# Layer 1's feed-forward in a two-layer latent backbone: where VectorE reads the high parts of weights, which engine splits the down weights, and when the second half's operands are made

## The chip, the core and the metric

The kernel runs on one NeuronCore of a Trainium2 chip. The metric is the device time of one execution in microseconds (us). A core has five engines that run side by side, each through its own list of instructions in order, and wait for each other on semaphores: TensorE (PE in the profile; its weight loads are PEld), VectorE (DVE), ScalarE (ACT), GpSimd (POOL) and SyncE (SP), which here does nothing but start transfers (DMAs) from memory. SBUF is the core's working memory; PSUM is the memory of eight banks into which TensorE accumulates, and which VectorE and ScalarE read and write as well.

## The reference

Two layers over 1024 latent tokens of width 1024 (and 256 context tokens). Each layer is a mixer and a feed-forward, with an RMS norm and a modulation by a conditioning vector ahead of each. Layer 0's mixer is Fourier mixing beside windowed attention, layer 1's is neighbourhood attention. The change is in layer 1's feed-forward, with a hidden width of 2816:

```
def _swiglu(h, wg, wu, wd):
    return (jax.nn.silu(h @ wg) * (h @ wu)) @ wd
...
h = _rms(x, norm2_g[i]) * (1.0 + sc2) + sh2
x = x + g2 * _swiglu(h, ffn_w_gate[i], ffn_w_up[i], ffn_w_down[i])
```

## The kernel before

**Precision.** Every matrix product is made of three: each operand is split in a high part (rounded to a short mantissa, type `F32R`) and a low part (what the rounding left), and `mm3` issues high by high, high by low and low by high (L74, L75, L76). So each weight tile needs a cast to the high part and a subtraction for the low one. In layer 1's feed-forward `parts_of` does this for a 128x512 block: ScalarE casts (`w_hi`, L1238), then VectorE, or GpSimd where told so, subtracts (`w_lo`, L1239). Both results lie in rings of 6 blocks.

**The stage.** It comes last in the kernel, behind layer 1's attention and its output projection (`out_proj1`). The 1024 tokens are worked in two halves (`ci` 0 and 1) of 512, and each half in 22 column blocks `f` of 128 hidden units.

For a block, `gate_up1` multiplies with gate and up weights together. The weights are seen as a two by two block matrix (`b11`, `b21` the two halves of the gate weights' rows, `b12`, `b22` those of the up weights), the activations too (two halves of tokens by two halves of the 1024 inputs), and the product is made of seven block products in place of eight (Winograd's form of Strassen's scheme). GpSimd forms four combinations of the raw weights (`t1` to `t4`, L1323, L1324, L1328, L1332; tiles named `t` in the profile, in a ring of 4). Seven weight operands (`b11`, `t2`, `t3`, `t1`, `t4`, `b21`, `b22`, in this order) go through `parts_of`, the last two with GpSimd as the subtracting engine. Each product (`product7`) is 12 matmuls into a PSUM tile `p_ps`, of which there are 4. ScalarE copies the first product to `p` (L1326); VectorE adds up the others (`u`, `av`, `sg`, L1330 to L1351), ScalarE applies SiLU, and the result is split in `act_hi` and `act_lo` (L1353, L1354). The activations' own seven combinations, `c_hi` and `c_lo`, are made once for each half by `combine`.

Two blocks make a pair. After each even `f` from 2 on, `down1` multiplies the pair before it with its down weights: 8 tiles `d_ps` of 6 matmuls each, which VectorE adds into `x` (L1379). The down weights of a block come in two halves, each a transfer to `wd_raw` (L1368, a ring of 2), a cast on ScalarE (L1369) and a subtraction on VectorE (L1370); the parts lie in the rooms `h_hi` and `h_lo` (one pair each), which held the mixer's output before.

The raw gate and up weights (`w_raw`, L1232, 512 KB each) have a ring of 4, so those of block `f` can be fetched only once the last reader of block `f - 2` is done: for the gate weights that is the `b21` subtraction, for the up weights the `b22` one, both on GpSimd. SP issues all these transfers in one list. It waits in place when a buffer isn't free, and what stands behind it waits too.

**The two halves.** The norm of the second half (`norm1s`, handed on as `own1`) is a generator: each `gate_up1` advances it by some steps, amid the first blocks of the first half. Its results go to memory (`h_d`) and come back as `h_in` for `combine` between the last two downs of the first half.

**What sets the order.** In this stage nobody writes out each engine's list. The language's scheduler makes it from the order of the code and its own costs, within the dependencies and the rings.

Of the kernel before, what the change touches and what calls it, by code (L numbers as in the profile page):

```python
# [9 lines left out]
F32 = mybir.dt.float32  # L10
# [6 lines left out]
P = 128  # L17
# [46 lines left out]
def build(tc, io):  # L64
# [4 lines left out]
    def fl(ap):  # L69
        return ap.bitcast(F32)  # L70
# [1152 lines left out]
    ww, ww_cm = pools.open("ring1", bufs=6)  # L1223
    wk, wk_cm = pools.open("wk1")
    pd, pd_cm = pools.open("pd1", bufs=3, psum=True)
    pm, pm_cm = pools.open("pm1", bufs=1, psum=True)
    pp, pp_cm = pools.open("pp1", bufs=4, psum=True)
    HT = 256

    def raw_weights(src):  # L1230
# [3 lines left out]

    def parts_of(src, eng=V):

        hi, lo = (ww.tile([P, 4, P], F32R, name=n) for n in ("w_hi", "w_lo"))
        S.copy(hi, src)  # L1238
        eng.tensor_tensor(lo, src, fl(hi), ALU.subtract)  # L1239
        return hi, lo  # L1240

    def out_weights(dt):
# [24 lines left out]
    def norm1s(ci, adder, done):  # L1267


        ts = slice(ci * 512, ci * 512 + 512)  # L1270
        ss = wk.tile([P, 512], F32, name="nrm_ss")
        for i, k in enumerate(reversed(range(KT))):
            if i == 0:
                S.activation(ss, x[:, k, ts], AF.Square)
            else:
                sq = wk.tile([P, 512], F32, name="nrm_sq", tag="t", bufs=4)
                S.activation(sq, x[:, k, ts], AF.Square)
                adder.tensor_tensor(ss, ss, sq, ALU.add)
            yield
        for r in norm_rstd(ss, 512, wk, pm):  # L1280
            yield
        for i in range(4):
            both = []
            for k in (i, i + 4):
                t = wk.tile([P, 512], F32, name="nrm_t", tag="t", bufs=4)
                V.scalar_tensor_tensor(t, x[:, k, ts], nA[3][:, k, 0:1], r, ALU.mult, ALU.mult)
                h = wk.tile([P, 512], F32, name="nrm_h", bufs=2)
                S.activation(h, t, AF.Identity, bias=vec(1, 3)[:, k, 0:1], scale=1.0)
                both.append(h)
                yield  # L1290
            done(i, *both)
            yield
# [1 line left out]

    M1, M2 = slice(0, HT), slice(HT, 2 * HT)

    def combine(i, h0, h4, pool=wk, tags=("act_hi", "act_lo")):

        s, r = (pool.tile([P, 2, HT], F32, name="s_sum", tag=t, bufs=4) for t in tags)
        G.tensor_tensor(s[:, 0], h0[:, M2], h4[:, M2], ALU.add)  # L1300
        G.tensor_tensor(s[:, 1], s[:, 0], h0[:, M1], ALU.subtract)
        G.tensor_tensor(r[:, 0], h0[:, M1], h0[:, M2], ALU.subtract)
        G.tensor_tensor(r[:, 1], h4[:, M1], s[:, 1], ALU.subtract)
        for sl, src in ((slice(0, 1), h0[:, M1].unsqueeze(1)),
                        (slice(1, 3), h4.rearrange("p (a n) -> p a n", a=2)), (slice(3, 5), s), (slice(5, 7), r)):
            S.copy(c_hi[:, sl, i], src)
            V.tensor_tensor(c_lo[:, sl, i], src, fl(c_hi[:, sl, i]), ALU.subtract)
# [7 lines left out]
    def gate_up1(f, side=iter(())):  # L1315
        g, u = raw_weights(io["w_gate"][1, f]), raw_weights(io["w_up"][1, f])
        b11, b21, b12, b22 = g[:, 0:4], g[:, 4:8], u[:, 0:4], u[:, 4:8]
        t1, t2, t3, t4 = (wk.tile([P, 4, P], F32, name=n, tag="t", bufs=4) for n in ("t1", "t2", "t3", "t4"))
        p1, u2, u3, sg = (wk.tile([P, HT], F32, name=n) for n in ("p1", "u2", "u3", "sg"))
        av = wk.tile([P, 2, HT], F32, name="av", bufs=2)  # L1320
        hi, lo = (wk.tile([P, 512], F32R, name=n, bufs=4) for n in ("act_hi", "act_lo"))
        w = parts_of(b11)
        G.tensor_tensor(t1, b12, b11, ALU.subtract)  # L1323
        G.tensor_tensor(t2, b22, t1, ALU.subtract)  # L1324
        ps = product7(w, 0)
        S.copy(p1, ps)  # L1326
        w = parts_of(t2)
        G.tensor_tensor(t3, b22, b12, ALU.subtract)  # L1328
        ps = product7(w, 4)
        V.tensor_tensor(u2, ps, p1, ALU.add)  # L1330
        w = parts_of(t3)
        G.tensor_tensor(t4, t2, b21, ALU.subtract)  # L1332
# [5 lines left out]
        V.tensor_tensor(u2, ps, u2, ALU.add)  # L1338
        w = parts_of(t4)
        ps = product7(w, 2)  # L1340
        V.tensor_tensor(u3, u3, ps, ALU.subtract)
# [4 lines left out]
        V.tensor_tensor(sg, ps, p1, ALU.add)  # L1346
        S.activation(sg, sg, AF.Silu)
        w = parts_of(b22, G)
        ps = product7(w, 6)
        V.tensor_tensor(u2, ps, u2, ALU.add)  # L1350
        V.tensor_tensor(av[:, 0], u2, sg, ALU.mult)  # L1351
        avf = av.rearrange("p a n -> p (a n)")
        S.copy(hi, avf)  # L1353
        V.tensor_tensor(lo, avf, fl(hi), ALU.subtract)  # L1354
        advance(side, 3)
        return hi, lo


# [4 lines left out]
    def down_weights1(f):  # L1363

        w_in = w_room[f // 2 % 2]
        for h in range(2):
            raw = wk.tile([P, 4, P], F32, name="wd_raw", bufs=2)
            nc.sync.dma_start(raw, io["w_down"][1, f][:, 4 * h:4 * h + 4])  # L1368
            S.copy(w_in[:, f % 2, h, 0], raw)  # L1369
            V.tensor_tensor(w_in[:, f % 2, h, 1], raw, fl(w_in[:, f % 2, h, 0]), ALU.subtract)  # L1370

    def down1(ci, fs, acts, last):
        w_in = w_room[fs[0] // 2 % 2]
        ts = slice(ci * 512, ci * 512 + 512)
        for dt in range(KT):
# [3 lines left out]
            V.scalar_tensor_tensor(x[:, dt, ts], ps, vec(1, 5)[:, dt, 0:1], x[:, dt, ts], ALU.mult, ALU.add)  # L1379
            if last:  # L1380
                nc.scalar.dma_start(io["out"][:, dt, ts], x[:, dt, ts])

    def keep(i, h0, h4):
        for k, h in ((i, h0), (i + 4, h4)):
# [11 lines left out]
    for ci in range(2):  # L1396
        acts = {}
        for f in range(NF):
            if f:
                down_weights1(f - 1)  # L1400
            acts[f] = gate_up1(f, own1)
            if f % 2 == 0 and 2 <= f < NF - 2:
                down1(ci, (f - 2, f - 1), [acts.pop(f - 2), acts.pop(f - 1)], False)
        down_weights1(NF - 1)
        for f in (NF - 4, NF - 2):
            down1(ci, (f, f + 1), [acts.pop(f), acts.pop(f + 1)], f == NF - 2)
            if f == NF - 4 and ci == 0:
                for i in range(4):
                    h = wr.tile([P, 2, 512], F32, name="h_in", tag="w_raw")
                    for n in range(2):  # L1410
                        nc.sync.dma_start(h[:, n], h_d[:, i + 4 * n])
                    combine(i, h[:, 0], h[:, 1], wr, ("w_raw", "w_raw"))
    pools.close(pp_cm, pm_cm, pd_cm, wk_cm, ww_cm, wr_cm, xp_cm, cc_cm, bg_cms[1], cst_cm)

# [109 lines left out]
```

## Time and profile before

| | |
|---|---|
| time, median of 3 runs | 2990.45 us (2989.44 to 2991.74) |
| the profiled execution | 2985.47 us; from first to last instruction 2983.6 us |
| mean granted TensorE clock | 0.988 of full speed |
| TensorE busy | 2837.0 us, 95% of the span |
| VectorE, ScalarE, GpSimd busy | 57%, 35%, 25% of the span |
| the stage: first block product to the end | 2190.6 to 2983.6 us |

The profile names an instruction by its line, its engine and its tiles, written out<-in. "Idle before" is the time in which the engine had nothing to do ahead of an instruction, with the instruction or transfer that released it. Over the whole kernel VectorE and GpSimd are far from full; in this stage VectorE is busy for 654 of 794 us. The stage falls into the blocks of the first half (to 2564 us), its last two downs (to 2597 us), the blocks of the second half (to 2957 us) and the last two downs.

### The profile page before, as it was taken

The page shows a single profiled execution, that of the slowest core. Times are in us where ns is not written, and L with a number is a line of the kernel's source. Part 1 is how long each engine was busy: PE and PEld are TensorE (multiplying, and loading weights), DVE is VectorE, ACT ScalarE, POOL GpSimd, SP SyncE. Part 2 cuts the span into 40 slices and gives each one's busy share as a digit, 9 for nine tenths or more (in the row PEclk, how much of TensorE's full clock was granted, in tenths as well). Part 3 has the DMA queues.
Part 4 walks back from the last instruction along what each step waited for, and adds up shares of the span by engine and source line. Part 5 has one row for each costly group of instructions (what it writes and reads, how often), then busy time and mean ns, then how long its engine had stood idle before and what let it go on. Part 6 is the DMA issues. An engine that isn't in the chain of part 4 may idle for free.

```text
span 2983.6 us, 43968 instructions
## 1 busy us (share of the span) xinstructions
PE 2837.0 (95%) x16874; PEld 2355.5 (79%) x16874; DVE 1692.7 (57%) x3172; ACT 1051.9 (35%) x2135; POOL 732.1 (25%) x738
## 2 busy tenths in 40 slices
PE   7989999999999999999989999999989899889999
PEld 5876768888888888888767887777778788778888
DVE  5775553622323333333575242666488787888887
ACT  4345552511111111111353232666354333433332
POOL 1112332000000000000220003554155454554452
PEclk9989999999999999999999999999999999999999
DMA  7236664111011111011134236873543222322221
GB/s 273 94 106 236 216 218 129 57 43 40 31 44 43 36 36 43 29 43 43 57 113 145 85 103 174 196 181 89 182 137 110 87 85 96 128 95 94 99 86 64
DMA packets 137698, 310.57 MB, mean 104 GB/s; under 512 B 11504, under 2 KB 69360, under 8 KB 130448
## 3 DMA queue, kind: packets, MB, share of 16 engines
q1 hardware_dynamic: 129056, 288.80, 30.7%
q0 software_dynamic: 1952, 8.32, 1.0%
q10 hardware_dynamic: 6480, 10.63, 1.0%
q8 instruction: 134, 2.20, 0.3%
q14 instruction: 76, 0.62, 0.1%
HBM read 264.58 MB, written 43.12 MB: 103 GB/s over the span
## 4 chain that ended last, share of the span: by engine, by line
PE 65%; DVE 15%; DMA 9%; issue 5%; ACT 4%; POOL 3%; SPq 0%; DVEq 0%; ACTq 0%; POOLq 0%
PE d_ps L74 6%; PE d_ps L75 6%; PE d_ps L76 6%; PE u_ps L75 4%; PE u_ps L76 4%; PE u_ps L74 4%; PE g_ps L76 4%; PE g_ps L74 4%; PE g_ps L75 4%; DVE w_lo L1239 4%; DMA wd_raw<-w_down 3%; PE pt_ps L589 3%; PE po L1170 2%; PE s_ps L599 2%; PE s_ps L600 2%
## 5 line engine op out<-in xcount | busy, mean ns | idle before, releaser
L74 PE MATMUL p_ps<-c_hi,w_hi 128*128 128x256 f32 x1232 | 353.5, 287 | 42.4 <-DVE u L1330 16.0
L76 PE MATMUL p_ps<-c_hi,w_lo 128*128 128x256 f32 x1232 | 346.0, 281 | 2.8 <-POOL w_lo L1239 1.7
L75 PE MATMUL p_ps<-c_lo,w_hi 128*128 128x256 f32 x1232 | 345.2, 280 | 0.0
L810 POOL TENSOR_TENSOR nrm_ss<-nrm_ss,nrm_sq 128x512 f32<-128x512 f32 (+1 forms) x31 | 39.3, 1269 | 1013.2 <-PE d_ps L76 935.6
L74 PEld LDWEIGHTS p_ps<-c_hi,w_hi 128*128 128x128 f32 x1232 | 234.9, 191 | 57.9 <-DVE u L1330 19.3
L775 ACT CAST w_hi<-w_raw 128x1024 fp32r<-128x1024 f32 x106 | 110.2, 1049 | 482.0 <-PE d_ps L75 270.5
L76 PEld LDWEIGHTS p_ps<-c_hi,w_lo 128*128 128x128 f32 x1232 | 234.3, 190 | 5.5 <-POOL w_lo L1239 4.0
L75 PEld LDWEIGHTS p_ps<-c_lo,w_hi 128*128 128x128 f32 x1232 | 234.6, 190 | 0.8
L878 DVE SCALAR_TENSOR_TENSOR x<-d_ps,mod,x 128x512 f32<-128x512 f32 (+1 forms) x240 | 157.6, 661 | 125.3 <-PE d_ps L76 125.3
L776 DVE TENSOR_TENSOR w_lo<-w_raw,w_hi 128x1024 fp32r<-128x1024 f32 x102 | 124.1, 1224 | 183.8 <-ACT w_hi L775 181.6
L580 POOL TENSOR_SCALAR pr<-pr,st 128x640 f32<-128x640 f32 (+2 forms) x208 | 156.0, 751 | 265.5 <-DVE st L579 173.5
L862 DVE TENSOR_TENSOR sg<-sg,u_ps 128x512 f32<-128x512 f32 (+1 forms) x66 | 39.5, 599 | 320.0 <-PE u_ps L76 320.0
L74 PE MATMUL d_ps<-act_hi,w_hi 128*128 128x512 f32 (+1 forms) x528 | 189.4, 359 | 3.4 <-DVE x L878 3.4
L75 PE MATMUL d_ps<-act_lo,w_hi 128*128 128x512 f32 (+1 forms) x528 | 189.3, 359 | 1.3 <-DVE act_lo L864 1.3
L76 PE MATMUL d_ps<-act_hi,w_lo 128*128 128x512 f32 (+1 forms) x528 | 189.4, 359 | 0.0
L75 PE MATMUL u_ps<-o_lo,w_hi 128*128 128x512 f32 (+1 forms) x528 | 188.6, 357 | 0.0
L76 PE MATMUL u_ps<-o_hi,w_lo 128*128 128x512 f32 (+1 forms) x528 | 188.6, 357 | 0.0
L74 PE MATMUL u_ps<-o_hi,w_hi 128*128 128x512 f32 (+1 forms) x528 | 188.5, 357 | 0.0
L74 PE MATMUL g_ps<-o_hi,w_hi 128*128 128x512 f32 (+1 forms) x528 | 188.5, 357 | 0.0
L76 PE MATMUL g_ps<-o_hi,w_lo 128*128 128x512 f32 (+1 forms) x528 | 188.5, 357 | 0.0
L75 PE MATMUL g_ps<-o_lo,w_hi 128*128 128x512 f32 (+1 forms) x528 | 188.4, 357 | 0.0
L574 ACT ACTIVATE pr<-sm,st 128x640 f32<-128x640 f32 (+4 forms) x208 | 162.7, 782 | 31.1 <-POOL sm L563 22.2
(320 smaller groups left out, 7371.3 us busy)
## 6 DMA issues: line engine op xcount, KB each, us to landing
ada_w<-ada_w SPq DMA_DIRECT2D x48, 1024.0 KB, 4.9
w_raw<-w_gate SPq DMA_DIRECT2D x66, 512.0 KB, 3.5
w_raw<-w_up SPq DMA_DIRECT2D x66, 512.0 KB, 4.0
wd_raw<-w_down SPq DMA_DIRECT2D x88, 256.0 KB, 3.1
k<-k_d SPq DMA_DIRECT2D x28, 640.0 KB, 10.3
w_raw<-w_out SPq DMA_DIRECT2D x32, 512.0 KB, 3.6
w_raw<-w_in SPq DMA_DIRECT2D x24, 512.0 KB, 4.0
w_raw<-w_down SPq DMA_DIRECT2D x22, 512.0 KB, 3.5
```

The costliest lines, as they stand in the source:

```text
L74: TE.matmul(out, lh, rh, start=first, stop=False)
L75: TE.matmul(out, lh, rl, start=False, stop=False)
L76: TE.matmul(out, ll, rh, start=False, stop=last)
L574: S.activation(self.pr[:, :n], self.sm[:, :n], AF.Exp, bias=st[:, 0:1], scale=-1.0, accum_out=st[:, 1:2])
L580: G.tensor_scalar(self.pr[:, :n], self.pr[:, :n], st[:, 3:4], 0.0, ALU.mult, ALU.add)
L589: TE.transpose(pt[:, b * P:(b + 1) * P], self.pr[:, (b0 + b) * P:(b0 + b + 1) * P], ident)
L599: TE.matmul(s_ps, q, k_hi[:, keys], start=True, stop=False)
L600: TE.matmul(s_ps, q, k_lo[:, keys], start=False, stop=True)
L775: S.copy(hi, raw)
L776: eng.tensor_tensor(lo, raw, fl(hi), ALU.subtract)
L878: V.scalar_tensor_tensor(xs, self.shaped(ps[:, :n]), vec(l, 5)[:, dt, v:v + 1], xs, ALU.mult, ALU.add)
L1239: eng.tensor_tensor(lo, src, fl(hi), ALU.subtract)
```

## The change

1. **High parts from PSUM.** Where VectorE makes the low part, ScalarE first copies the high part once more, into a PSUM tile (`pmisc`, 2 buffers; the profile of the changed kernel will call the copy's line L1243), and VectorE's subtraction (L1244) takes one operand from PSUM and one from SBUF, where both came from SBUF before. GpSimd's subtractions of `b21` and `b22` stay as they were. To make room, the products `p_ps` have 3 PSUM buffers in place of 4, and the norm's scratch tile moves to the new pool.
2. **Down weights on GpSimd.** The low parts of the down weights (now L1375) are subtracted by GpSimd in place of VectorE: 88 instructions on 128x512 blocks, 4 for each pair.
3. **The second half's norm.** It is advanced by 2 steps for each block, not 3, and from block 1 on, not from block 0.
4. **The second half's operands.** The loads of `h_in` are issued ahead of the last two downs of the first half, and `combine` runs amid them, after their second and sixth tiles, with its scratch in the ring `t`.

```diff
-    pm, pm_cm = pools.open("pm1", bufs=1, psum=True)
-    pp, pp_cm = pools.open("pp1", bufs=4, psum=True)
+    pp, pp_cm = pools.open("pp1", bufs=3, psum=True)
+    ph, ph_cm = pools.open("ph1", bufs=2, psum=True)
...
         S.copy(hi, src)
-        eng.tensor_tensor(lo, src, fl(hi), ALU.subtract)
+        first = fl(hi)
+        if eng is V:
+            first = ph.tile([P, 512], F32, name="pmisc").rearrange("p (k n) -> p k n", n=P)
+            S.copy(first, fl(hi))
+        eng.tensor_tensor(lo, src, first, ALU.subtract)
...
-        for r in norm_rstd(ss, 512, wk, pm):
+        for r in norm_rstd(ss, 512, wk, ph):
...
-    def combine(i, h0, h4, pool=wk, tags=("act_hi", "act_lo")):
+    def combine(i, h0, h4, tags=("act_hi", "act_lo")):
-        s, r = (pool.tile([P, 2, HT], F32, name="s_sum", tag=t, bufs=4) for t in tags)
+        s, r = (wk.tile([P, 2, HT], F32, name="s_sum", tag=t, bufs=4) for t in tags)
...
-        advance(side, 3)
+        advance(side, 2)
...
             S.copy(w_in[:, f % 2, h, 0], raw)
-            V.tensor_tensor(w_in[:, f % 2, h, 1], raw, fl(w_in[:, f % 2, h, 0]), ALU.subtract)
+            G.tensor_tensor(w_in[:, f % 2, h, 1], raw, fl(w_in[:, f % 2, h, 0]), ALU.subtract)
-    def down1(ci, fs, acts, last):
+    def down1(ci, fs, acts, last, amid=lambda dt: None):
...
+            amid(dt)
...
-            acts[f] = gate_up1(f, own1)
+            acts[f] = gate_up1(f, own1 if f else iter(()))
...
         down_weights1(NF - 1)
+        h_in = []
+        for i in range(4 if ci == 0 else 0):
+            h_in.append(wr.tile([P, 2, 512], F32, name="h_in", tag="w_raw"))
+            for n in range(2):
+                nc.sync.dma_start(h_in[i][:, n], h_d[:, i + 4 * n])
+        def amid(dt):
+            if dt % 4 == 1 and h_in:
+                h = h_in.pop(0)
+                combine(3 - len(h_in), h[:, 0], h[:, 1], tags=("t", "t"))
         for f in (NF - 4, NF - 2):
-            down1(ci, (f, f + 1), [acts.pop(f), acts.pop(f + 1)], f == NF - 2)
-            if f == NF - 4 and ci == 0:
-                for i in range(4):
-                    h = wr.tile([P, 2, 512], F32, name="h_in", tag="w_raw")
-                    for n in range(2):
-                        nc.sync.dma_start(h[:, n], h_d[:, i + 4 * n])
-                    combine(i, h[:, 0], h[:, 1], wr, ("w_raw", "w_raw"))
+            down1(ci, (f, f + 1), [acts.pop(f), acts.pop(f + 1)], f == NF - 2, amid)
```

**How the order moves.** Below are pieces of three engines' lists from the steady part of a half, before and after. A row is a line, an operation, out<-in and a shape; "x4" is four in a row. Take as C the odd block whose seven products come right behind a down, and as E the even block after it.

GpSimd before, one pair: the four combinations of a coming block, then the `b21` and `b22` low parts of an earlier one, twice.

```order
L1323 TENSOR_TENSOR t_22470<-w_raw 128x512
L1324 TENSOR_TENSOR t_22471<-w_raw,t_22470 128x512
L1328 TENSOR_TENSOR t_22472<-w_raw 128x512
L1332 TENSOR_TENSOR t_22473<-t_22471,w_raw 128x512
L1239 TENSOR_TENSOR w_lo<-w_raw,w_hi 128x512 x2
L1323 TENSOR_TENSOR t_22630<-w_raw 128x512
L1324 TENSOR_TENSOR t_22631<-w_raw,t_22630 128x512
L1328 TENSOR_TENSOR t_22632<-w_raw 128x512
L1332 TENSOR_TENSOR t_22633<-t_22631,w_raw 128x512
L1239 TENSOR_TENSOR w_lo<-w_raw,w_hi 128x512 x2
```

GpSimd after, one pair:

```order
L1328 TENSOR_TENSOR t_21682<-w_raw 128x512
L1329 TENSOR_TENSOR t_21683<-w_raw,t_21682 128x512
L1333 TENSOR_TENSOR t_21684<-w_raw 128x512
L1337 TENSOR_TENSOR t_21685<-t_21683,w_raw 128x512
L1244 TENSOR_TENSOR w_lo<-w_raw,w_hi 128x512
L1375 TENSOR_TENSOR h_lo<-wd_raw,h_lo 128x512 x4
L1244 TENSOR_TENSOR w_lo<-w_raw,w_hi 128x512
L1328 TENSOR_TENSOR t_21916<-w_raw 128x512
L1329 TENSOR_TENSOR t_21917<-w_raw,t_21916 128x512
L1333 TENSOR_TENSOR t_21918<-w_raw 128x512
L1337 TENSOR_TENSOR t_21919<-t_21917,w_raw 128x512
L1244 TENSOR_TENSOR w_lo<-w_raw,w_hi 128x512 x2
```

The four splits of the pair's down weights stand between C's `b21` and C's `b22`.

SP before, then after: `w_gate` and `w_up` of one block, with the down weights' four transfers.

```order
L1232 DMA w_raw<-w_gate 128x1024
L1368 DMA wd_raw<-w_down 128x512 x3
L1232 DMA w_raw<-w_up 128x1024
L1368 DMA wd_raw<-w_down 128x512
L1232 DMA w_raw<-w_gate 128x1024
L1232 DMA w_raw<-w_up 128x1024
```

```order
L1232 DMA w_raw<-w_gate 128x1024
L1373 DMA wd_raw<-w_down 128x512 x4
L1232 DMA w_raw<-w_up 128x1024
L1232 DMA w_raw<-w_gate 128x1024
L1232 DMA w_raw<-w_up 128x1024
```

All four now stand ahead of the `w_up` transfer. Through the ring of 2, the first of the four waits for the pair's first split on GpSimd, the second for the second split, and the third and fourth (which belong to the next pair) for the third and fourth.

ScalarE before, then after, from E's `act_hi`, while TensorE runs the down, to C's copy `p` and past it.

```order
L1353 CAST act_hi<-av 128x512
L1369 CAST h_lo<-wd_raw 128x512 x3
L1238 CAST w_hi<-w_raw 128x512
L1326 COPY p_21322<-p_ps 128x256
L1369 CAST h_lo<-wd_raw 128x512
L1238 CAST w_hi<-w_raw 128x512
L1238 CAST w_hi<-t_21479 128x512
```

```order
L1358 CAST act_hi<-av 128x512
L1374 CAST h_hi<-wd_raw 128x512 x4
L1331 COPY p_21112<-p_ps 128x256
L1239 CAST w_hi<-w_raw 128x512 x2
L1243 COPY pmisc<-w_hi 128x512
L1239 CAST w_hi<-t_21279 128x512
L1243 COPY pmisc<-w_hi 128x512
```

All four casts of down weights now stand ahead of `p`, and the cast of C's `b22` stands behind it. With 3 buffers of `p_ps`, C's fourth product waits for that copy.

More of the change, by code (lines that the diff above doesn't have):

```diff
@@ L1404, in build @@
         down_weights1(NF - 1)
-        for f in (NF - 4, NF - 2):
-            down1(ci, (f, f + 1), [acts.pop(f), acts.pop(f + 1)], f == NF - 2)
-            if f == NF - 4 and ci == 0:
-                for i in range(4):
-                    h = wr.tile([P, 2, 512], F32, name="h_in", tag="w_raw")
-                    for n in range(2):
-                        nc.sync.dma_start(h[:, n], h_d[:, i + 4 * n])
-                    combine(i, h[:, 0], h[:, 1], wr, ("w_raw", "w_raw"))
-    pools.close(pp_cm, pm_cm, pd_cm, wk_cm, ww_cm, wr_cm, xp_cm, cc_cm, bg_cms[1], cst_cm)
+        h_in = []
[7 more added lines that the diff above has]
+                combine(3 - len(h_in), h[:, 0], h[:, 1], tags=("t", "t"))
+        for f in (NF - 4, NF - 2):
+            down1(ci, (f, f + 1), [acts.pop(f), acts.pop(f + 1)], f == NF - 2, amid)
+    pools.close(ph_cm, pp_cm, pd_cm, wk_cm, ww_cm, wr_cm, xp_cm, cc_cm, bg_cms[1], cst_cm)
 def _split11(a):
```

## The prediction

> **What bounds the kernel now.** I read the page first, then the time by stages, the waits of each engine within the stage, and last the timelines of GpSimd, SP and ScalarE over one pair. The page's slices (first row: TensorE's busy tenths in 40 of them) show TensorE full almost everywhere, so the stage itself has to be opened. The columns of the other rows are the stretch, its length, the busy time of TensorE, its weight loads, VectorE, ScalarE and GpSimd, the granted clock, and the share and rate of the transfers.
>
> ```profile
> PE   7989999999999999999989999999989899889999
> ```
>
> ```profile
> 2190.00:2277.00 87.00, 69.29 (x485) 64.48 (x486) 76.48 (x108) 44.24 (x84) 52.37 (x34) 0.92 0.42 137
> 2554.00:2638.00 84.00, 68.02 (x429) 60.09 (x429) 70.03 (x100) 34.64 (x68) 49.19 (x40) 0.94 0.38 127
> 2638.00:2957.00 319.00, 301.01 (x2033) 266.92 (x2032) 267.65 (x395) 122.37 (x243) 159.65 (x110) 0.99 0.26 86
> 2451.72:2485.98 34.26, 32.21 (x218) 28.38 (x217) 28.83 (x43) 13.08 (x26) 17.50 (x12) 1.00 0.27 91
> ```
>
> The long steady stretch of the second half runs at 0.99 clock with TensorE busy for 94% of it; the start (2190 to 2277) and the turn between the halves (2554 to 2638) lose more: 17.7 and 16.0 us of idle TensorE, and clock too. The last row is one pair of blocks: 34.26 us with TensorE busy for 32.21, so about 2 us of each pair are waits. VectorE has 28.83 us of work in it, GpSimd 17.50.
>
> The waits of TensorE, GpSimd and SP from 2190 us to the end (us in total, times, longest):
>
> ```profile
> PE d_ps L74 <- DVE x L1379: 17.8, 17, 6.3
> PE p_ps L74 <- DVE u L1330: 16.0, 16, 2.2
> PE p_ps L74 <- ACT p L1326: 11.5, 20, 1.9
> PE pmisc L164 <- DVE nrm_ss L1278: 7.3, 1, 7.3
> POOL t L1323 <- DMA w_raw<-w_up: 131.3, 26, 6.5
> POOL w_lo L1239 <- ACT w_hi L1238: 125.1, 39, 7.3
> SPq L1232 <- POOL w_lo L1239: 436.0, 65, 12.8
> ```
>
> TensorE's waits are short ones on VectorE and ScalarE. But why do the pairs keep 34.3 us? GpSimd is half idle, and yet it waits 131 us for the up weights and 125 us for casts, while SP stands 436 us behind GpSimd's `w_lo`. Each waits for the other: that is a loop. One turn of it, on GpSimd, SP and ScalarE (start, duration, instruction, idle before it):
>
> ```profile
> 2459.63 1.74 POOL L1239 TENSOR_TENSOR w_lo<-w_raw,w_hi 128x512 fp32r<-128x512 f32 x1
> 2467.36 1.29 POOL L1239 TENSOR_TENSOR w_lo<-w_raw,w_hi 128x512 fp32r<-128x512 f32 x1 [6.00 <-ACT w_hi L1238]
> 2473.68 1.59 POOL L1323 TENSOR_TENSOR t<-w_raw 128x512 f32<-128x512 f32 x1 [5.03 <-DVE u L1338]
> 2479.09 1.28 POOL L1332 TENSOR_TENSOR t<-t,w_raw 128x512 f32<-128x512 f32 x1 [0.69 <-DVE w_lo L1239]
> 2482.17 1.32 POOL L1239 TENSOR_TENSOR w_lo<-w_raw,w_hi 128x512 fp32r<-128x512 f32 x1 [0.38 <-ACT w_hi L1238]
> 2487.98 1.62 POOL L1323 TENSOR_TENSOR t<-w_raw 128x512 f32<-128x512 f32 x1 [4.49 <-DVE sg L1346]
> 2493.93 1.74 POOL L1239 TENSOR_TENSOR w_lo<-w_raw,w_hi 128x512 fp32r<-128x512 f32 x1
> 2501.87 1.29 POOL L1239 TENSOR_TENSOR w_lo<-w_raw,w_hi 128x512 fp32r<-128x512 f32 x1 [6.19 <-ACT w_hi L1238]
> ```
>
> ```profile
> 2461.81 7.75 SPq L1368 DMA_DIRECT2D wd_raw<-w_down  x3
> 2469.65 0.38 SPq L1232 DMA_DIRECT2D w_raw<-w_up  x1
> 2483.52 0.33 SPq L1232 DMA_DIRECT2D w_raw<-w_up  x1
> ```
>
> ```profile
> 2465.61 1.14 ACT L1369 CAST h_hi<-wd_raw 128x512 fp32r<-128x512 f32 x2 [7.92 <-DMA wd_raw<-w_down]
> 2466.66 0.62 ACT L1238 CAST w_hi<-w_raw 128x512 fp32r<-128x512 f32 x1
> 2467.18 0.36 ACT L1326 COPY p<-p_ps 128x256 f32<-128x256 f32 x1
> ```
>
> C's `b21` ends at 2461.37 and frees a buffer; SP issues down transfers at 2461.81, ScalarE's two casts wait for them until 2465.61, C's `b22` cast stands behind these, and so GpSimd's `b22` ends only at 2468.65. That frees the up weights' buffer; their issue, behind a third down transfer, comes at 2469.65, and `t` begins at 2473.68. Four combinations and E's `b21` and `b22` follow to 2483.49; the next up transfer is issued at 2483.52, `t` begins at 2487.98, and the next `b21` ends at 2495.67: 34.3 us after the first. No link of it is TensorE. This loop sets the pair's time, and VectorE is close behind.
>
> **The change, part by part.**
>
> *Down splits on GpSimd, with all four down transfers ahead of the up transfer.* The loop's prices, from the rows above and these (two transfers with their median time to landing, in the stage; then the down transfers' least, median and greatest; then groups from 2310 to 2548 us):
>
> ```profile
> w_raw<-w_up SPq DMA_DIRECT2D x43, 512.0 KB, 4.3
> DMA to landing us min/median/max: 2.4/3.1/6.1
> L1328 POOL TENSOR_TENSOR t<-w_raw 128x512 f32<-128x512 f32 x14 | 22.2, 1586 | 0.0
> L1323 POOL TENSOR_TENSOR t<-w_raw 128x512 f32<-128x512 f32 x14 | 20.9, 1493 | 71.6 <-DMA w_raw<-w_up 46.5 <-DVE u L1341 5.7 <-DVE w_lo L1239 5.4
> L1324 POOL TENSOR_TENSOR t<-w_raw,t 128x512 f32<-128x512 f32 x14 | 20.7, 1479 | 1.1
> L1332 POOL TENSOR_TENSOR t<-t,w_raw 128x512 f32<-128x512 f32 x14 | 18.6, 1331 | 3.5 <-DVE w_lo L1239 3.5
> L1239 POOL TENSOR_TENSOR w_lo<-w_raw,w_hi 128x512 fp32r<-128x512 f32 x26 | 37.6, 1449 | 45.2 <-ACT w_hi L1238 45.2
> L1239 DVE TENSOR_TENSOR w_lo<-t,w_hi 128x512 fp32r<-128x512 f32 x55 | 48.1, 874 | 0.0
> L1370 DVE TENSOR_TENSOR h_hi<-wd_raw,h_hi 128x512 fp32r<-128x512 f32 x16 | 17.6, 1102 | 23.1 <-ACT h_hi L1369 23.1
> ```
>
> A split on GpSimd has no row. Its nearest is GpSimd's `w_lo`, the same operation on 128x512 from SBUF: 1.29 alone (2467.36, 2501.87), 1.45 in the mean. Behind C's `b21`, four splits now stand ahead of `b22`. The first frees a buffer; a transfer is issued and lands; a cast; the second split; another transfer, another cast; the fourth split (the third runs meanwhile); `b22`. I take 3 x 1.29 + 2 landings of 2.8 (between the least 2.4 and the median 3.1, as little else is in flight then) + 2 casts of 0.57 + 1.29 + 0.4 of handovers (0.08 between a cast's end and GpSimd, five times) = 12.3 us from `b21`'s end to `b22`'s. Before it was 2468.65 - 2461.37 = 7.3: +5.0. Given back: the up issue no longer stands behind a down transfer, 1.0 us (2468.65 to 2469.65).
>
> *High parts from PSUM.* What it can bring the loop is in GpSimd's durations. Its combinations take 1.33 to 1.59 in the mean against 1.28 alone (2479.09): they are slowed while VectorE works on two SBUF operands, as its `w_lo` does for 0.87 us at a time. Eleven of the pair's twelve GpSimd instructions lie in the loop outside `b22`: 2 x (1.59 + 1.49 + 1.48 + 1.33) + 3 x 1.5 = 16.3 us, against 14.1 at 1.28, and 1.1 us of idle between them (0.69 and 0.38). So the relief lies between 0 and 3.3; I take 2.0, as VectorE keeps three operations a block on two SBUF operands (`av` twice, `act_lo`). The loop comes to 34.3 + 5.0 - 1.0 - 2.0 = 36.3, **+2.0 us a pair**. From below: landings of 2.4 and full relief, 34.3 + 4.2 - 1.0 - 3.3 = 34.2. From above: splits at 1.45, a first landing of 3.7 (2461.81 to the cast at 2465.61), a second of 3.1, relief 1.0: 34.3 + 6.6 - 1.0 - 1.0 = 38.9.
>
> VectorE loses 4 splits of about 1.1 us a pair, from 28.8 to about 24. Off the loop this buys nothing by itself. ScalarE gets 10 copies into PSUM a pair. No row shows one; the nearest is its cast of the same block, 0.57 to 0.62, so about +6 on the 13.08 of the pair's row, off the path even at twice that. TensorE then waits where the order shows it: C's fourth product needs `p`, behind the four casts. By the walk `p` comes some 10 us after C's `b21` (12.3 less 1.29 for `b22` and 1.29 for the last split), where the down and three products cover about half.
>
> The steady stretches, 2277 to 2554 and 2638 to 2957, hold 596 us or 17 pairs; I count 16, since the first ones run from weights loaded ahead: +32 us (-2 to +74).
>
> *Three buffers of `p_ps`.* Their only price is the wait for `p` above, already counted. Without that wait a fourth product would stand behind `p` in place of the fifth behind `u`, 0.36 us of copy against 16.0 us in 16 times: between -1 and 0 a pair, and 0 as long as the loop is longer.
>
> *Norm of the second half from block 1 on.* TensorE's 7.3 us wait for `nrm_ss` goes, with the half clock behind it. Three rows of clock, and two of TensorE's timeline that stand ahead of the second and third:
>
> ```profile
> 2200.20:2207.50 7.30, 7.30 (x34) 7.30 (x35) 4.01 (x6) 5.18 (x12) 5.92 (x5) 0.50 0.38 127
> 2249.00:2252.00 3.00, 3.00 (x8) 2.33 (x9) 1.90 (x4) 0.62 (x1) 2.92 (x3) 0.50 0.73 244
> 2573.00:2579.80 6.80, 4.70 (x11) 3.74 (x12) 6.44 (x10) 2.86 (x7) 3.59 (x5) 0.50 0.49 154
> 2248.78 0.79 PE L74 MATMUL d_ps<-act_hi,h_hi 128*128 128x512 f32 x1 [4.12 <-DVE x L1379]
> 2575.10 0.80 PE L74 MATMUL d_ps<-act_hi,h_lo 128*128 128x512 f32 x1 [6.31 <-DVE x L1379]
> ```
>
> At clock 0.50 over 7.3 us, half the work is lost: 3.7 us. But block 0's second operand is still late, for the up weights and GpSimd come first, and the norm's steps return over the next blocks. Bounds: -11 (all gone) and +5 (a like wait later, less the fast part); I take -5.
>
> *Operands amid the last downs.* At the turn TensorE waits 6.31 us for `x` behind `combine`'s work on VectorE, then runs 6.8 us at half clock (3.4 lost), and the stretch holds 16.0 us idle. With the operands made earlier, block 0 of the second half finds its weights ready. But SP's loads of `h_in` wait for GpSimd's last `w_lo`, and VectorE's `c_lo` stands ahead of the last block's additions, which TensorE waits for. Bounds -18 and 0; I take -10.
>
> Sum: 32 - 5 - 10 = +17 on the profiled execution's 2985.47, which is 5.0 under the median of the runs shown: **3007** against 2990.45.
>
> **The rivals.**
>
> *The loop isn't longer, and VectorE's relief counts.* If transfers land quickly and the splits fall into GpSimd's waits, the pair goes down to TensorE's own busy time, 32.2 us: 16 x -2.1 = -34, with -15 at the ends: 2941. For it: GpSimd is idle for 17 us of a pair and VectorE was at 84%. Against it: GpSimd's idle time is the loop's own waiting, and two transfers in a row now lie in it. It decides where `b21` to `b22` takes 8.2 us or less (10.3 would leave the pair at 34.3). Halfway lies the low bound, 34.2 a pair: 2990.45 - 2 - 15 = 2973.
>
> *The loop is at its upper bound*, 38.9 a pair: +74 - 15 = 3049. For it: a landing of 3.7 in the very turn shown.
>
> *No change.* With +0.9 a pair the ends pay for it: +14 - 15 = 2990.
>
> *The clock drops in each pair.* A TensorE wait of over 4 us in each pair may be followed by half clock: the rows above show it behind waits of 7.3, 4.1 and 6.3 us, and waits around 2 us (the `u` and `p` rows) leave the pair shown at 1.00. At 36.3 a pair against 32.2 busy, all of TensorE's waits come to 4.1, of which `p`'s may be 3 to 4: at the edge. A stretch of 3 us at half clock costs 1.5, and the slack of the loop takes it first, since the next `p` wait is the shorter by it; if it pays only half and the ends add some, +1.0 a pair: 3023. The Trainium skill, TensorE: Matmul & The Clock Gate, in its table of rules, says that no idle gap over about 3 us should lie between bursts of matmuls, as one window of idle sends the clock back to half. By that rule each pair would pay, and the sum would be this rival's 3023; the trace agrees from 4.1 us up, and no quoted wait lies between 2.2 and 4.1.
>
> *The PSUM copies hold up VectorE.* With only 2 buffers, ScalarE's copy waits for VectorE, and with it all behind it. ScalarE's slack, about 15 us a pair with the copies, speaks against it; at 1 us a pair on top of the forecast it gives 3023 as well.
>
> **How the numbers follow.** Forecast, loop at 35.5 to 37.5 a pair (2994 to 3026): 0.42. Clock 0.06, copies 0.03. Upper bound: 0.11. No change: 0.12. Low loop (2973): 0.13. TensorE's own time (2941): 0.13. So faster 0.26, same 0.12, slower 0.62, where 0.2% or 6 us is about what the runs can tell from no change. Leaving out the lower half of the 2941 case and the top of the 3049 one, the range is 2950 to 3045; that of the forecast alone is 2994 to 3026.
>
> **What would show it.** Right: from `b21` to `b22` on GpSimd around 12 us with the splits between, the next up transfer issued right behind `b22`, pairs of about 36 us, TensorE's longest waits on `p` (L1331) some 3 to 5 us once a pair, VectorE with idle time, its `w_lo` below 0.87 and GpSimd's combinations near 1.3. The norm's 7.3 us and the turn's 6.3 us waits shorter. Wrong: down transfers that land while GpSimd still has other work, so that splits follow one another; or pairs near 32 us with TensorE's waits gone.

## The result and the profile after

The changed kernel takes 3015.12 us (median of 4 runs, 3014.64 to 3019.57) against 2989.94 us (2988.40 to 2991.74): a ratio of 1.0087, 95% interval 1.0070 to 1.0105. It is slower, by 25 us; 3007 was forecast. The profiled execution took 3014.64 us with a span of 3012.9.

The steady part of the stage by stretches (first half, turn, second half; the columns are those of the prediction's first fence):

```profile
2314.00:2532.00 218.00, 196.33 (x1297) 180.45 (x1297) 134.67 (x230) 115.42 (x218) 127.90 (x96) 0.94 0.27 87
2532.00:2647.00 115.00, 100.25 (x651) 90.81 (x650) 78.47 (x133) 65.97 (x128) 76.37 (x64) 0.95 0.36 120
2647.00:2942.00 295.00, 265.73 (x1729) 244.84 (x1729) 178.90 (x301) 152.41 (x286) 170.59 (x128) 0.92 0.26 86
```

VectorE has fallen to 179 of 295 us in the second half, where it had 268 of 319. It was relieved, as the change has it, and yet TensorE's busy share is down from 94% to 90%, at a clock of 0.92. The waits tell where:

```profile
PE p_ps L74 <- ACT p L1331: 58.1, 18, 5.2
PE p_ps L74 <- ACT w_hi L1239: 8.1, 2, 7.6
POOL h_hi L1375 <- ACT h_hi L1374: 66.2, 22, 5.5
POOL h_lo L1375 <- ACT h_lo L1374: 49.0, 16, 5.8
SPq L1373 <- POOL h_hi L1375: 75.8, 46, 9.3
SPq L1373 <- POOL h_lo L1375: 66.2, 39, 6.7
```

TensorE now waits 58 us for the copy `p`, 18 times, where it had 11.5 us in 20. GpSimd waits 115 us for casts ahead of its new splits, and SP stands 142 us before down transfers behind those splits. One round of the loop, on GpSimd, SP and ScalarE:

```profile
2466.36 1.30 POOL L1244 TENSOR_TENSOR w_lo<-w_raw,w_hi 128x512 fp32r<-128x512 f32 x1
2467.61 1.30 POOL L1375 TENSOR_TENSOR h_hi<-wd_raw,h_hi 128x512 fp32r<-128x512 f32 x1
2473.01 2.52 POOL L1375 TENSOR_TENSOR h_hi<-wd_raw,h_hi 128x512 fp32r<-128x512 f32 x2 [4.10 <-ACT h_hi L1374]
2477.49 1.29 POOL L1375 TENSOR_TENSOR h_hi<-wd_raw,h_hi 128x512 fp32r<-128x512 f32 x1 [1.95 <-ACT h_hi L1374]
2478.73 1.28 POOL L1244 TENSOR_TENSOR w_lo<-w_raw,w_hi 128x512 fp32r<-128x512 f32 x1
2484.21 1.44 POOL L1328 TENSOR_TENSOR t<-w_raw 128x512 f32<-128x512 f32 x1 [4.19 <-DVE w_lo L1244]
2490.11 2.57 POOL L1244 TENSOR_TENSOR w_lo<-w_raw,w_hi 128x512 fp32r<-128x512 f32 x2
2502.68 1.29 POOL L1244 TENSOR_TENSOR w_lo<-w_raw,w_hi 128x512 fp32r<-128x512 f32 x1
```

```profile
2468.94 10.19 SPq L1373 DMA_DIRECT2D wd_raw<-w_down  x4
2480.04 0.33 SPq L1232 DMA_DIRECT2D w_raw<-w_up  x1
```

```profile
2472.32 1.14 ACT L1374 CAST h_hi<-wd_raw 128x512 fp32r<-128x512 f32 x2 [7.34 <-DMA wd_raw<-w_down]
2476.79 0.62 ACT L1374 CAST h_hi<-wd_raw 128x512 fp32r<-128x512 f32 x1 [3.33 <-DMA wd_raw<-w_down]
2477.32 0.36 ACT L1331 COPY p<-p_ps 128x256 f32<-128x256 f32 x1
```

C's `b21` ends at 2467.66. The first split follows, and with it the first transfer goes out; its cast stands at 2472.32. Second and third split, second transfer, a cast at 2476.79, fourth split, and only then `b22`, which ends at 2480.01. That is 12.35 us where there were 7.28. It is so in every round of the loop in the steady stretches: 12.2 to 13.0 us, against 7.2 to 8.6 before. The up transfer goes out 0.03 us later, not 1.0. The next `b21` begins at 2502.68, 36.32 us after this one.

### The profile page after: what moved, and what is told of

Its sections match the earlier page's. It is cut to its first block, busy times and chain, and to the rows that moved or that the text cites. A ratio compares the mean times of both kernels' runs of the same rounds, so it can differ in the third digit from the quotient of the medians.

```text
span 3012.9 us, 44371 instructions
## 1 busy us (share of the span) xinstructions
PE 2848.3 (95%) x16874; PEld 2383.4 (79%) x16874; DVE 1550.6 (51%) x3084; ACT 1200.7 (40%) x2390; POOL 809.7 (27%) x826
## 5 line engine op out<-in xcount | busy, mean ns | idle before, releaser
L74 PE MATMUL p_ps<-c_hi,w_hi 128*128 128x256 f32 x1232 | 364.5, 296 | 75.9 <-ACT p L1331 58.1
L76 PE MATMUL p_ps<-c_hi,w_lo 128*128 128x256 f32 x1232 | 358.7, 292 | 6.6 <-DVE w_lo L1244 3.4
L75 PE MATMUL p_ps<-c_lo,w_hi 128*128 128x256 f32 x1232 | 358.7, 291 | 0.0
L74 PEld LDWEIGHTS p_ps<-c_hi,w_hi 128*128 128x128 f32 x1232 | 249.2, 202 | 84.5 <-ACT p L1331 62.5
L76 PEld LDWEIGHTS p_ps<-c_hi,w_lo 128*128 128x128 f32 x1232 | 248.3, 202 | 8.1 <-DVE w_lo L1244 4.1
L75 PEld LDWEIGHTS p_ps<-c_lo,w_hi 128*128 128x128 f32 x1232 | 249.8, 203 | 0.9
L574 ACT ACTIVATE pr<-sm,st 128x640 f32<-128x640 f32 (+4 forms) x208 | 162.7, 782 | 31.1 <-POOL sm L563 22.3
```

The costliest lines, as they stand in the source:

```text
L74: TE.matmul(out, lh, rh, start=first, stop=False)
L75: TE.matmul(out, lh, rl, start=False, stop=False)
L76: TE.matmul(out, ll, rh, start=False, stop=last)
L574: S.activation(self.pr[:, :n], self.sm[:, :n], AF.Exp, bias=st[:, 0:1], scale=-1.0, accum_out=st[:, 1:2])
```

## The experiments

To compare them I take the time of a pair: the distance of the first matmuls of two downs in TensorE's timeline, over the pairs between, the last six of the first half and eight of the second. Before, the second half's are those at 2638.59 and 2913.99: 275.4 us for eight. All ratios are to the kernel before.

| kernel | median us | ratio, 95% interval | pair us, first and second half |
|---|---|---|---|
| before | 2989.94 | | 35.0, 34.4 |
| the change | 3015.12 | 1.0087 (1.0070 to 1.0105) | 36.3, 36.9 |
| `splits_back` | 2949.05 | 0.9858 (0.9843 to 0.9873) | 32.4, 33.0 |
| `only_splits` | 3050.71 | 1.0202 (1.0187 to 1.0217) | 37.7, 37.8 |
| `ring4` | 2910.62 | 0.9731 (0.9717 to 0.9746) | 30.9, 30.4 |
| `norm_and_turn` | 2993.99 | 1.0014 (1.0002 to 1.0025) | 34.4, 34.6 |
| `nrm_shared` | 3022.06 | 1.0116 (1.0099 to 1.0133) | 36.0, 36.8 |
| `before_ring4` | 2931.97 | 0.9810 (0.9792 to 0.9829) | 30.7, 31.6 |
| `four_p_ps` | 3019.46 | 1.0107 (1.0092 to 1.0122) | 36.4, 36.6 |
| `ring4_norm_back` | 2914.39 | 0.9755 (0.9739 to 0.9771) | 30.8, 30.3 |
| `before_ring4_turn` | 2936.50 | 0.9828 (0.9813 to 0.9843) | 31.7, 31.0 |
| `ring4_splits_back` | 2910.37 | 0.9735 (0.9719 to 0.9751) | 31.1, 30.8 |
| `ring4_only_splits` | 2946.76 | 0.9858 (0.9841 to 0.9875) | 31.6, 31.4 |

**The splits, back on VectorE and alone on GpSimd.** `splits_back` is the change with

```diff
-            G.tensor_tensor(w_in[:, f % 2, h, 1], raw, fl(w_in[:, f % 2, h, 0]), ALU.subtract)
+            V.tensor_tensor(w_in[:, f % 2, h, 1], raw, fl(w_in[:, f % 2, h, 0]), ALU.subtract)
```

> The change with the down weights' low parts back on VectorE; all else as changed (PSUM copies, 3 p_ps buffers, norm and operands moved). Theory A (the loop GpSimd - SP - transfer - ScalarE got longer because four splits and two transfers in a row stand between b21 and b22): b21 to b22 falls back from 12.3 to about 7.3 us, GpSimd keeps its shorter combinations, so the pair of blocks goes from 36.2 to 36.9 us down to 32.4 to 33.5, and the time to 2960 to 2978 us, faster than before. Rival B (the PSUM copies, ScalarE in front of VectorE with two buffers, or three p_ps buffers, make the pair longer): pairs stay near 36 us, 3005 to 3015 us.

`only_splits` is the kernel before with the opposite edit.

> The kernel before with nothing but the down weights' low parts on GpSimd. Theory A: b21 to b22 takes about 12.3 us here too, the four down transfers stand ahead of the up transfer, and GpSimd's combinations are not relieved, as VectorE still reads two SBUF operands; pairs of 36.5 to 38.5 us, time 3025 to 3055 us, slower than the whole change. Rival B: this part costs little, pairs near 34.4 us, 2985 to 2998 us.

Without the splits on GpSimd the change is worth 41 us; with them alone, the kernel loses 61. In GpSimd's timeline, first of `splits_back` (`b21` and `b22`), then of `only_splits` (`b21`, four splits, `b22`):

```profile
2442.56 1.30 POOL L1244 TENSOR_TENSOR w_lo<-w_raw,w_hi 128x512 fp32r<-128x512 f32 x1
2450.17 1.68 POOL L1244 TENSOR_TENSOR w_lo<-w_raw,w_hi 128x512 fp32r<-128x512 f32 x1 [6.32 <-ACT w_hi L1239]
```

```profile
2755.74 1.29 POOL L1239 TENSOR_TENSOR w_lo<-w_raw,w_hi 128x512 fp32r<-128x512 f32 x1
2756.99 1.28 POOL L1370 TENSOR_TENSOR h_hi<-wd_raw,h_hi 128x512 fp32r<-128x512 f32 x1
2762.61 2.51 POOL L1370 TENSOR_TENSOR h_hi<-wd_raw,h_hi 128x512 fp32r<-128x512 f32 x2 [4.34 <-ACT h_hi L1369]
2767.10 1.28 POOL L1370 TENSOR_TENSOR h_hi<-wd_raw,h_hi 128x512 fp32r<-128x512 f32 x1 [1.98 <-ACT h_hi L1369]
2768.34 1.29 POOL L1239 TENSOR_TENSOR w_lo<-w_raw,w_hi 128x512 fp32r<-128x512 f32 x1
```

8.0 us from the end of `b21` to that of `b22` in the first, 12.6 in the second; over all steady rounds 7.2 to 8.1 and 12.1 to 13.8. The distance follows the splits, whatever else is in the kernel, and rival B of both expectations falls: the PSUM copies, together with the 3 buffers of `p_ps`, are no cost but the gain. The time of `splits_back` lies 11 us under the low end expected.

**Four buffers for the down weights.** `ring4` is the change with

```diff
-                h = wk.tile([P, 512], F32, name="nrm_h", bufs=2)
+                h = wk.tile([P, 512], F32, name="nrm_h", tag="t", bufs=4)
...
-            raw = wk.tile([P, 4, P], F32, name="wd_raw", bufs=2)
+            raw = wk.tile([P, 4, P], F32, name="wd_raw", bufs=4)
```

The first edit only makes room for the second. The order of the four splits between `b21` and `b22` is the same as in the change; on ScalarE the cast of C's `b22` now stands ahead of `p`.

> The change with 4 buffers for wd_raw in place of 2 (the room comes from nrm_h, which shares the ring t). The order of the four splits between b21 and b22 stays, but no split has to wait for a transfer that an earlier split released. Theory A: b21 to b22 falls to 6.5 to 8.5 us (four splits, b22 and a wait for the last cast), pairs to 32.3 to 33.8 us, time 2950 to 2980 us. Rival B (PSUM copies or p_ps buffers): pairs stay near 36.5 us and the time within 5 us of the change's 3015. Rival C (the sheer work of four splits on GpSimd, not the transfers in a row): pairs near 35 us, 2995 to 3005 us.

GpSimd's timeline from `b21` to `b22`, and the steady stretch of the first half:

```profile
2434.53 1.30 POOL L1244 TENSOR_TENSOR w_lo<-w_raw,w_hi 128x512 fp32r<-128x512 f32 x1
2435.79 2.54 POOL L1375 TENSOR_TENSOR h_hi<-wd_raw,h_hi 128x512 fp32r<-128x512 f32 x2
2438.55 2.55 POOL L1375 TENSOR_TENSOR h_hi<-wd_raw,h_hi 128x512 fp32r<-128x512 f32 x2 [0.22 <-PE d_ps L75]
2441.04 1.32 POOL L1244 TENSOR_TENSOR w_lo<-w_raw,w_hi 128x512 fp32r<-128x512 f32 x1
```

```profile
2303.00:2489.00 186.00, 185.71 (x1301) 168.79 (x1301) 138.21 (x230) 117.78 (x217) 129.09 (x96) 1.00 0.34 104
```

The four splits run one behind another, 6.5 us from `b21`'s end to `b22`'s (6.2 to 6.5 over all steady rounds), since their transfers had landed long before, by 2413.2. TensorE is busy for 185.71 of 186 us at full clock. So it was not the splits' work on GpSimd but the two transfers in a row between them. Each of these waited for a buffer that the split before it freed. 2910.62 us is under both kernels, 79 us under before, and 39 us under the low end expected; the pairs, too, are shorter than the 32.3 us expected. How much of the 79 us is the change's, the kernel before with the same buffers shows (`before_ring4`, below).

**Control of the room.** `nrm_shared` has only the first of the two edits.

> Control for the run with 4 wd_raw buffers: the change with nrm_h in the ring t, and still 2 buffers for wd_raw. Theory A (two transfers in a row inside the loop cost the time, and the 4 buffers took them out): no effect, 3010 to 3020 us, pairs near 36.5 us. Rival: the room made for the buffers, or the other order of the norm that it brings, is part of the gain; then it lies under 3005 us.

3022: 2 us above the expected bounds, and no gain. The four buffers made all of `ring4`'s gain over the change.

**Four buffers without the change.** `before_ring4` is the kernel before with both edits of `ring4`.

> The kernel before with 4 buffers for wd_raw (room again from nrm_h), nothing else: splits on VectorE, both operands from SBUF. Theory A (a late down transfer ahead of b22's cast, and a down transfer ahead of the up transfer, were part of the loop before as well): b21 to b22 falls from 7.3 to about 5 us, pairs from 34.4 to 31.5 to 33.0 us, 2945 to 2970 us; the rest to the change with 4 buffers is what VectorE's and GpSimd's relief brings. Rival (without the relief of VectorE the buffers bring nothing): pairs 34 to 34.5 us, 2985 to 2995 us.

2932, 13 us under the low end expected. GpSimd's `b21` and `b22`, and the second half:

```profile
2445.49 1.75 POOL L1239 TENSOR_TENSOR w_lo<-w_raw,w_hi 128x512 fp32r<-128x512 f32 x1
2450.50 1.30 POOL L1239 TENSOR_TENSOR w_lo<-w_raw,w_hi 128x512 fp32r<-128x512 f32 x1 [3.27 <-ACT w_hi L1238]
```

```profile
2612.00:2865.00 253.00, 249.53 (x1729) 223.48 (x1729) 229.37 (x337) 110.71 (x208) 142.56 (x96) 1.00 0.32 101
```

4.6 us from end to end instead of 7.3 (3.0 to 6.3 over all steady rounds, 6.3 in most of the second half). With two more buffers, VectorE at 229 of 253 us and no relief, the pairs fall to 30.7 and 31.6 us: the loop, not VectorE, was the bound before. The order moved a little too: in the round shown, all four down transfers now stand ahead of the up transfer, and all four casts ahead of `p`, as in the change. So that order alone doesn't make the loop long. Of the 79 us by which `ring4` is under before, 58 come with the buffers alone; with four buffers in both kernels the change is worth 21.

**The buffers of the products.** `four_p_ps` is the change with

```diff
-    pd, pd_cm = pools.open("pd1", bufs=3, psum=True)
+    pd, pd_cm = pools.open("pd1", bufs=2, psum=True)
-    pp, pp_cm = pools.open("pp1", bufs=3, psum=True)
+    pp, pp_cm = pools.open("pp1", bufs=4, psum=True)
```

> The change with 4 buffers for p_ps as before (and 2 for d_ps in place of 3, since PSUM is full). TensorE's longest wait in the change is the fourth product's for the copy p. Theory A (that wait is the loop seen from TensorE): the wait moves to the fifth product, pairs stay at 36 to 37.5 us, time 3005 to 3025 us. Rival (the three buffers make the wait, and with it the half clock that follows): pairs fall below 35 us, time below 2995 us.

TensorE's waits in it:

```profile
PE p_ps L74 <- ACT p L1331: 47.4, 21, 3.7
PE d_ps L74 <- DVE x L1384: 16.1, 19, 3.2
```

The wait for `p` shrank from 58.1 to 47.4 us and moved as expected: in the change it stands ahead of the fourth product behind a down (17 times), here ahead of the fifth (16 times). Other waits took its place, the pairs stayed, and `b21` to `b22` still takes 12.2 to 14.0 us. The wait is the loop seen from TensorE. (The one `d_ps` buffer given up has a price of its own, 16.1 us of waits there against 4.0 in the change; the run doesn't separate it.)

**The norm and the turn.** `norm_and_turn` is the kernel before with parts 3 and 4 of the change; `ring4_norm_back` is `ring4` with part 3 undone; `before_ring4_turn` is `before_ring4` with parts 3 and 4.

> The kernel before with only the norm's steps moved (from block 1 on, 2 steps a block) and the second half's operands made amid the last downs. In the trace of the change the start gave 3 us back but began 5 us later, and the turn gave 3. Theory A (the prediction's -15 for the two was too much): 2984 to 2992 us. Rival (the two are worth what was predicted, and the PSUM copies or splits took it back in the change): 2970 to 2978 us.

> The change with 4 wd_raw buffers, and the norm of the second half as before (from block 0, 3 steps a block); the operands stay amid the last downs. Pairs as with 4 buffers, 30.4 to 30.9 us. If the prediction's term for the norm holds (a gain of 5 us), undoing it costs 5: 2912 to 2920 us. If the norm's move is what made the output projection 4 us longer in every kernel that has it, undoing it is even or a gain: 2902 to 2911 us.

> The kernel before with 4 wd_raw buffers and with the norm's steps and the second half's operands moved as in the change (no PSUM copies, splits on VectorE). With 2 buffers this move was worth nothing (2994 against 2990). Theory A (the move's gain at the turn is hidden as long as the loop on GpSimd sets the pace on both sides of it): with 4 buffers it gains 5 to 12 us on 2932, so 2920 to 2927 us, with the turn shortened from 114 to 106 to 110 us. Rival (it is worth nothing in any case): 2928 to 2938 us.

Alone the two parts gain nothing: 2993.99, 2 us above what was expected. The norm's wait is still there (the row below, of `norm_and_turn`); in the change its place is taken by block 0's second operand, 7.6 us on `w_hi` in the change's waits above.

```profile
PE pmisc L164 <- DVE nrm_ss L1278: 8.2, 1, 8.2
```

Undoing the norm's move in `ring4` costs 3.8 us, inside what a gain of 5 from the move would give, but the intervals overlap; no verdict. The output projection, which makes its weights' parts with `parts_of` as well, takes 98.7 us there, from its first matmul at 2095.66 to the first block product at 2194.36. That is as in the change, against 94.7 before, so in these two kernels the norm's move doesn't make the 4 us. `norm_and_turn` has them too (98.6), but at another place: the tenth of the projection's 16 tiles takes 10.3 us there and 7.2 before, while in the change it is the first (8.5 against 6.0) and the fifteenth (8.4 against 6.0). What makes them stays open. With four buffers, the two parts alone again gained nothing (2936.50 against 2931.97, and the turn 114.2 us in both): my theory for them, that the loop hid their gain, fell.

**The splits' place without the loop.** `ring4_splits_back` is `ring4` with the splits on VectorE, `ring4_only_splits` is `only_splits` with `ring4`'s two edits.

> The change with 4 wd_raw buffers and the splits of the down weights back on VectorE; PSUM copies, norm and turn as changed. Theory A (with the transfers out of the loop, TensorE is the bound of the pairs either way; moving the splits off VectorE brings little more): pairs of 30.4 to 31.0 us, 2905 to 2920 us. Rival (the splits on GpSimd are part of what makes the run with 4 buffers so fast): pairs over 31.2 us, 2920 to 2930 us.

> The kernel before with 4 wd_raw buffers and the splits on GpSimd, and nothing else. With 2 buffers the splits alone cost 61 us. Theory A (what they cost was the two transfers in a row; four splits of 1.3 us are only work): b21 to b22 about 7 us, GpSimd's combinations still slowed by VectorE, the loop near 32 to 33.5 us a pair, 2945 to 2975 us, some 80 to 100 us less than with 2 buffers. Rival (the splits' work on GpSimd itself is too much without VectorE's relief): pairs over 35 us, 3000 us or more.

With four buffers and the PSUM copies it doesn't matter who splits, 2910.37 against 2910.62. And the splits alone, which cost 61 us with two buffers, take 104 us less with four: 2946.76, with 6.2 to 7.3 us from `b21` to `b22`. Both times lie where theory A had them; the pairs miss its bounds a little (31.1 us against 31.0 at most, and 31.4 to 31.6 against 32 at least). But without the copies the splits on GpSimd still cost 15 us, 2946.76 against the 2931.97 of `before_ring4`, with intervals that don't meet. Of these, the pairs of the first half hold some 6 and the turn 3 (117.4 against 114.2); what makes them stays open.

## Why the prediction was right

The forecast of 3007 with a loop of 36.3 us a pair met 3015 and 36.32 in the round shown; 36.3 in the first half, 36.9 in the second. By its steps:

- **The loop sets the pair's time.** Shown: `before_ring4` takes waits for a down buffer out of that loop, leaves every engine's work as it was, and is 58 us faster.
- **12.3 us from `b21` to `b22`.** Measured 12.35 in the round shown, 12.2 to 13.0 over all steady rounds. The three unknowns fell near the values taken: a split takes 1.28 in the mean (below), the first transfer's cast begins 3.4 us after the split that released it ends (2468.91 to 2472.32), the second's 2.5 after its split (2474.3 to 2476.79). (The bound from above adds up to 6.7 us more, not 6.6; nothing hangs on it.)
- **Splits +4.0 a pair net of the up transfer's advance, 64 us.** Measured by taking them out: 3015.12 - 2949.05 = 66. By the pairs it is 3.9 each, and 14 such pairs make 55; the rest lies at the ends, 8.5 us at the turn, where the forecast had put nothing for the splits.
- **Relief -2.0 a pair, 32 us.** The PSUM copies (with 3 `p_ps` buffers), by `norm_and_turn` against `splits_back`: 2993.99 - 2949.05 = 45. In the pairs it is 2.0 in the first half (34.4 to 32.4) and 1.6 in the second, near the 2.0 taken; 14 such pairs make 25. The rest lies at the ends, where the forecast had put no relief: in the profiled executions the turn is 10.1 us shorter, and the way from the first block product to the first steady down 15.8 (126.4 to 110.6), out of 50 between the two. Groups of the change, 2310 to 2548 us:

```profile
L1243 ACT COPY pmisc<-w_hi 128x512 f32<-128x512 f32 x64 | 37.8, 591 | 2.0
L1244 DVE TENSOR_TENSOR w_lo<-t,pmisc 128x512 fp32r<-128x512 f32 x52 | 35.6, 685 | 9.8 <-ACT pmisc L1243 9.8
L1375 POOL TENSOR_TENSOR h_hi<-wd_raw,h_hi 128x512 fp32r<-128x512 f32 x14 | 17.8, 1284 | 22.0 <-ACT h_hi L1374 22.0
L1328 POOL TENSOR_TENSOR t<-w_raw 128x512 f32<-128x512 f32 x13 | 17.1, 1316 | 58.0 <-DMA w_raw<-w_up 21.8 <-DVE u L1355 9.6 <-DVE w_lo L1244 8.4
L1329 POOL TENSOR_TENSOR t<-w_raw,t 128x512 f32<-128x512 f32 x13 | 18.4, 1418 | 1.0
L1333 POOL TENSOR_TENSOR t<-w_raw 128x512 f32<-128x512 f32 x13 | 18.5, 1423 | 0.0
L1337 POOL TENSOR_TENSOR t<-t,w_raw 128x512 f32<-128x512 f32 x13 | 18.3, 1405 | 0.0
L1244 POOL TENSOR_TENSOR w_lo<-w_raw,w_hi 128x512 fp32r<-128x512 f32 x26 | 35.2, 1362 | 0.0
```

VectorE's `w_lo` went from 874 to 685 ns. Of GpSimd's four combinations three got shorter (1493 to 1316, 1479 to 1418, 1586 to 1423) and one longer (1331 to 1405), and its `w_lo` went from 1449 to 1362. In the two rounds shown (here and in the prediction), GpSimd's eleven instructions of the loop outside `b22` took 16.4 us before and 15.3 in the change, and the 1.1 us of idle between them went: so half of the relief is shorter instructions and half is waits for VectorE and for a cast. The copy into PSUM, which had no row, takes 591 ns, inside what was assumed.

- **The norm -5 and the turn -10.** This is the term that was mis-sized. Alone the two moves measured +4, so it was 19 us off; with 2 more for the splits and 13 less for the relief, that leaves the 8 us by which the forecast fell short. That these errors take each other back in part is luck. For the norm, the step that failed was that TensorE's wait for it would go: in `norm_and_turn`, with no other edit, it is 8.2 us instead of 7.3, and the way from the first block product to the first steady down is 126.4 us instead of 120.0. For the turn, the wait did go: of the 6.31 us for `x`, none over 3.0 is left in the turn of `norm_and_turn`. What failed was to take its length, and the half clock behind it, for time won. The turn, from the last steady down of the first half to the first of the second, before, in `norm_and_turn` and in `splits_back`:

```profile
2520.51:2638.59 118.08, 101.06 (x650) 89.05 (x649) 98.92 (x143) 47.73 (x94) 67.50 (x52) 0.96 0.34 117
2528.76:2645.26 116.50, 102.66 (x650) 89.65 (x649) 100.34 (x145) 48.23 (x96) 67.75 (x52) 0.94 0.36 118
2500.61:2607.05 106.44, 95.92 (x651) 85.27 (x649) 91.01 (x143) 64.99 (x125) 63.79 (x52) 1.00 0.40 128
```

The moves gave 1.6 us, with VectorE as busy as before and the clock no better. The copies, which took 9 us of work off VectorE there, gave 10.1; that VectorE's work bounds the turn is what these rows suggest, no run shows it alone. In the change the turn is 114.9: the splits on GpSimd took 8.5 back. So the 10 us were there, but belonged to another edit, and were spent at the same place.
- **TensorE's own time of 32.2 us a pair** was no floor: `ring4` runs pairs in 30.4. The busy time of a row holds modelled ends, and as a pair has the same matmuls in both kernels, part of the 32.2 were waits. It changed no term of the sum, but the rival built on it was too slow, and so were the bounds of three expectations (`splits_back`, `ring4`, `before_ring4`).
- **The half clock at the turn** was read too high, in the forecast's reasons for the -10: of the 6.8 us at clock 0.50 TensorE was busy for 4.70 by the row itself, so 2.4 us were lost there, not 3.4.
- **The clock.** In the change half clock follows 14 of the 15 waits of 2.8 us or more for `p`. One of them, with the stretch behind it, and the one without:

```profile
2477.74 0.58 PE L74 MATMUL p_ps<-c_hi,w_hi 128*128 128x256 f32 x1 [2.80 <-ACT p L1331]
2477.80:2481.00 3.20, 3.20 (x15) 3.20 (x16) 1.75 (x4) 3.11 (x6) 2.21 (x2) 0.50 0.22 85
2960.69 0.38 PE L74 MATMUL p_ps<-c_hi,w_hi 128*128 128x256 f32 x1 [2.81 <-ACT p L1331]
2960.70:2966.00 5.30, 5.28 (x44) 5.11 (x45) 3.83 (x9) 5.11 (x10) 2.30 (x2) 1.00 0.30 100
```

Two of the kernel before, at its turn:

```profile
2608.84 0.36 PE L74 MATMUL p_ps<-c_hi,w_hi 128*128 128x256 f32 x1 [3.16 <-DVE u L1334]
2608.90:2613.00 4.10, 3.88 (x31) 3.71 (x32) 4.10 (x7) 2.50 (x6) 2.88 (x2) 1.00 0.42 132
2620.28 0.38 PE L74 MATMUL p_ps<-c_hi,w_hi 128*128 128x256 f32 x1 [1.95 <-ACT p L1326]
2620.80:2624.10 3.30, 3.30 (x17) 3.30 (x17) 3.30 (x9) 1.50 (x3) 0.00 (x0) 0.50 0.87 313
```

So the length of one wait doesn't decide: half clock followed 1.95 us once, where TensorE had been idle for 6.6 of the last 24.7 us (2596.0 to 2620.7), and didn't follow 3.16. There is no sharp edge at the 3 to 4 us taken, and the pair by which the prediction held waits around 2 us harmless has none over 0.6. The Trainium skill (TensorE: Matmul & The Clock Gate, its table of rules) says that no idle gap over about 3 us should lie between bursts of matmuls. The trace agrees with it as a rough rule only. The price of that rival, 16 us more, wasn't paid as such: the first half's pairs came out at the forecast's 36.3 with the clock at 0.94. Over the eight pairs of the second half, `nrm_shared` has a clock of 0.94 and pairs of 36.8 us, `four_p_ps` 0.96 and 36.6, the change 0.92 and 36.9: the clock can't have made much of it. How much is open; no run took the clock alone away.

## What to carry to other kernels

Where an engine is half idle and still everything waits, follow one buffer from its release to the next release: the sum of that walk, transfers included, is the time of a round, and as long as no other round is longer, what is moved into it costs time, however idle its engine. Moving a consumer to another engine also moves the moment at which its buffer is freed; where that put two transfers in a row, two more buffers were worth 104 us, 58 of which the kernel before could have had without any of the change. And a stall at a boundary between stages is not yet time to be won: here the order that took it away gave 1.6 us, and the edit that took work off the engine it named gave 10.1.

## What the runs showed of the hardware

VectorE's subtraction of 128x512 takes 685 ns in the mean with one operand in PSUM, and never over 691 in the change's stage. With both in SBUF, beside a busy GpSimd, the mean is 874 ns, but the least is 673 and the longest 1752: the place of the operand matters only in part of the cases. GpSimd's own operations got shorter by 0.06 to 0.18 us in the mean, but for one that got longer by 0.07. TensorE's clock fell to half behind a wait of 1.95 us in one place, with more waits shortly before it, and not behind one of 3.16 in another; where it fell, it stayed there for at least 3.2 us (2477.8 to 2481).
